# A two-layer decoder trunk on one core: another order of the MLP's first products, stores on other queues, one product earlier, one row turned later

## The chip, the cores and the metric

The kernel runs on one core of a Trainium2 chip. The core has TensorE (PE, matrix products), VectorE (DVE), ScalarE (ACT), GpSimd (POOL) and SyncE (SP, which here only issues DMAs). Each engine runs its own instructions in their order and waits for others by semaphores. The metric is the device time of one execution in microseconds (us), as the median of several.

## The reference

Two layers on 1024 tokens of width 1024. Layer 0 mixes tokens by attention (differential and forgetting heads), layer 1 by a gated linear recurrence. The change touches what follows the mixer in both:

```python
h = h + rmsnorm(m, ln_mix_post[layer])          # m: the mixer's output
u = rmsnorm(h, ln_mlp_pre[layer])
f = jnp.square(jax.nn.relu(u @ mlp_w_up[layer])) @ mlp_w_down[layer]   # 1024 -> 4096 -> 1024
h = h + rmsnorm(f, ln_mlp_post[layer])
e = rmsnorm(p[layer] @ ple_w_proj[layer], ple_norm[layer])
h = h + e * jax.nn.sigmoid(h @ ple_w_gate[layer])
```

## The kernel before

**Numbers.** Every float32 operand of a product is split into a high part (a cast on ACT, L122) and a low part (a subtraction on DVE, L123). `mm3` (L154 to L156) issues three matmuls per product: high by high, high by low, low by high. A weight is thus ready for its first matmul when ACT has cast it (`wAh`) and for its second when DVE has subtracted (`wAl`).

**The MLP** is computed with seven block products instead of eight: tokens, features and hidden columns are halved, and sums of blocks are multiplied. The names A11, A12, A22, S1 to S4 are weight blocks or sums of them; B11, B21, B22, T1 to T4 are the matching factors on the other side. `vec` (L887) makes the sums on DVE.

**End of the mixer** (`mix_out`, a plan written out by hand). `out_row` makes a row block of 128 tokens: product, norm, residual, norm. `combine` transposes it on PE and splits it and its combinations. In the gaps of the plan stand the *leads*: the first two products, A11 and A12, of the first three *Quads* (a Quad is 512 hidden columns), each 24 matmuls. For a Quad q, `first()` runs A11 into a bank and copies the bank on ACT (L1097); `second()` lets A12 add into the same bank and squares the result on ACT (L1080, L1081), and SP stores it (L1103). I call the halves a1, a2 (Quad 0), b1, b2, c1, c2; the prediction's c11 and c12 are c1 and c2. `early_sums` prepares S1 and S2 of Quad 0.

**Up stage** (`mlp_up`). For each of eight Quads the remaining products run (S1, S2, S4, S3, A22, or all seven). `keep` (L1152) stores each finished block of hidden values, 512 KB, in HBM (`hidD`): the three B blocks from ACT's squares, the four T blocks from DVE's subtractions. All stores and all loads go through SP's queue, in one order.

**Down stage** (`mlp_down`). Four chunks of two Quads each. `step` loads the hidden blocks into tiles `c` (L1267), splits them, and splits the weights; A22's weights for a chunk lie in one tile (`w22`, seen as `uh` in the trace). The seven products of a chunk run in the order A11, A12, S2, S3, A22, S1, S4 on two pairs of banks (`k0` to `k3`); `onto` adds a bank to the result X on DVE, in the first chunk it copies it on ACT (L1318); `temp` copies a bank to a tile M. In the last chunk `norms` (through `add_norm`) normalises finished rows and adds h, loaded by SP, and `turns` transposes them (L190) for the gate.

**Gate** (in `mlp_and_ple`). The product with the gate weights goes over eight row blocks: the first four, those normalised in `mlp_down`, first. `need_u` turns a row that isn't turned yet.

A scheduler orders each engine's instructions from the program's text before it runs. Its order is fixed on the chip.

Of the kernel before, what the change touches and what calls it, by code (L numbers as in the profile page):

```python
# [39 lines left out]
def tile_hybrid_trunk(  # L40
# [870 lines left out]
    class Layer:  # L911
# [6 lines left out]

        def add_norm(self, tb, g, a, ag, src, junk, small):

            h = row_tile()
            nc.sync.dma_start(out=h, in_=src)
            rs = rms_row(small, junk, a)
            vec(ag, a, g, ALU.mult)
            nc.vector.scalar_tensor_tensor(out=h, in0=ag, scalar=rs, in1=h, op0=ALU.mult, op1=ALU.add)
            return h


        def mix_out(self, wap, kpairs, src, part, order):
# [11 lines left out]
            with tc.tile_pool(name=f"pre{layer}", bufs=1, reuse_waits="tile") as mp:  # L941
# [66 lines left out]

                leads = []
                for q in range(NLEAD):  # L1010
                    leads += self.lead_steps(q, mp)
                plan = [(out_row, 0), (out_row, 1), (out_row, 2), (combine, 0), (out_row, 3), (combine, 1),
# [70 lines left out]
        def lead_steps(self, q, mp):  # L1083

            A = self.loader(self.up_view(q), lambda m, k: (wpool, "wraw", 2))
            slot = [mp if 2 * q < 3 else None, mp if 2 * q + 1 < 3 else None]
            st = {}

            def direct(name, n):
                wh, wl = self.weights({name: lambda: A(0, n)}, name, A, None, slot[n])  # L1090
                return wh, wl

            def first():
                a = st["A"] = pair_bank()
                self.up_product(a, direct("A11", 0), "A11", True, True)
                self.lead[q] = m1 = self.c.take()
                nc.scalar.copy(out=m1[1], in_=a)  # L1097

            def second():
                self.up_product(st["A"], direct("A12", 1), "A12", False, True)  # L1100
                c11 = row_tile()
                self.squared(c11, st["A"])
                nc.sync.dma_start(out=self.hidD[B11][q], in_=c11)  # L1103

            return [first, second]
# [9 lines left out]
        def mlp_up(self):  # L1115
            quads = FF // 512
            layer_ = self
            with tc.tile_pool(name=f"up{self.layer}", bufs=1, reuse_waits="tile") as hp:
# [10 lines left out]
                class Quad:  # L1129
# [21 lines left out]
                    def keep(self, i, t):  # L1151
                        nc.sync.dma_start(out=layer_.hidD[i][self.q], in_=t)  # L1152

# [135 lines left out]
        def mlp_down(self, macc, bank0, norms, turns):  # L1289
# [8 lines left out]
            for c in range(chunks):  # L1298
# [29 lines left out]
                for jj, b in product("A12", 1, True):  # L1328
                    onto((0, 0), jj, b)
                for jj, b in product("S2", 0, False):  # L1330
                    temp("u2", jj, b)
                    if c:
                        onto((1, 0), jj, M["u2", jj])
                for jj, b in product("S3", 0, False):
                    temp("u3", jj, b)
                    if c:
                        onto((1, 1), jj, M["u3", jj])
                for jj, b in product("A22", 0, False):
                    onto((0, 1), jj, b, True)
                    if final:  # L1340
# [8 lines left out]
                for jj, b in product("S4", 1, False):  # L1349
# [4 lines left out]
                    if final:  # L1354
                        turns(2 - jj)
            return rows

        def mlp_and_ple(self):
# [21 lines left out]
            normed = []  # L1380

            def norms(tbs, rows):
                if not gain:
# [3 lines left out]
                    quart[TA, 0] = (uh0, ul0)  # L1387
                    gain.append(macc.tile([P, 2, 512], F32, name="M", bufs=6).rearrange("p r d -> p (r d)"))
                for tb in tbs:
                    a = rows[tb]  # L1390
                    h = self.add_norm(tb, gain[0], a, a, hD[tb], gain[1], mp)
                    nc.sync.dma_start(out=hD[tb], in_=h)
                    normed.append((tb, h))

            def turns(n):
                for _ in range(n):
                    tb, h = normed.pop(0)
                    to_u(tb, h, self.down_bank(tb % 2))

# [13 lines left out]
            for nh in range(2):  # L1413
# [6 lines left out]
                for n, tb in enumerate(order):  # L1420
# [4 lines left out]
                    if nh == 0:  # L1425
                        need_u([order[n + 3]] if 1 <= n < 5 else [])
                    else:
                        drain(1)
# [81 lines left out]
```

## Time and profile before

| what | us |
|---|---|
| median of three runs | 2670.49 (2666.25 to 2670.78) |
| the profiled execution | 2666.86 |
| its span, first to last instruction | 2665.0 |
| PE busy in the span | 2512.3 (94%) |
| DVE, ACT, POOL busy | 1664.4, 1265.7, 221.1 |

The mean granted TensorE clock of the span is 0.976 of full speed. All times "at" in the rows are microseconds from the span's start. "Idle before" is the time in which an engine did nothing ahead of an instruction, and behind the arrow stands what released it. The touched places lie, in layer 0, at 736 to 770 (leads' end), 1050 to 1075 (start of the down stage) and 1350 to 1380 (turn to the gate); in layer 1, 1932 to 1966, 2236 to 2266 and 2540 to 2570.

### The profile page before, as it was taken

The page shows a single profiled execution, that of the slowest core. Times are in us where ns is not written, and L with a number is a line of the kernel's source. Part 1 is how long each engine was busy: PE and PEld are TensorE (multiplying, and loading weights), DVE is VectorE, ACT ScalarE, POOL GpSimd, SP SyncE. Part 2 cuts the span into 40 slices and gives each one's busy share as a digit, 9 for nine tenths or more (in the row PEclk, how much of TensorE's full clock was granted, in tenths as well). Part 3 has the DMA queues.
Part 4 walks back from the last instruction along what each step waited for, and adds up shares of the span by engine and source line. Part 5 has one row for each costly group of instructions (what it writes and reads, how often), then busy time and mean ns, then how long its engine had stood idle before and what let it go on. Part 6 is the DMA issues. An engine that isn't in the chain of part 4 may idle for free. (4 is left out here: it accounts for less than half of the span.)

```text
span 2665.0 us, 31196 instructions
## 1 busy us (share of the span) xinstructions
PE 2512.3 (94%) x11681; PEld 2046.6 (77%) x11681; DVE 1664.4 (62%) x2085; ACT 1265.7 (47%) x1867; POOL 221.1 (8%) x310
## 2 busy tenths in 40 slices
PE   8899999987889999999989999999889998999999
PEld 7687988765668887788877778877678886788877
DVE  5566766663777456677775455663876546677763
ACT  4455555653634445444443356662634444434431
POOL 1312223311100000000010000000100000000010
PEclk9999999999899999999999999999999999999999
DMA  4747543414655346444454322144655437444453
GB/s 160 204 140 209 154 141 115 151 68 182 233 166 206 135 157 246 150 150 142 142 197 143 126 83 71 59 144 170 241 178 182 150 135 257 153 150 142 146 186 111
DMA packets 231259, 417.91 MB, mean 157 GB/s; under 512 B 17075, under 2 KB 127772, under 8 KB 231108
## 3 DMA queue, kind: packets, MB, share of 16 engines
q1 hardware_dynamic: 215556, 393.37, 44.5%
q10 hardware_dynamic: 15552, 22.55, 2.3%
q8 instruction: 92, 1.51, 0.2%
q14 instruction: 59, 0.48, 0.1%
HBM read 290.40 MB, written 125.45 MB: 156 GB/s over the span
## 5 line engine op out<-in xcount | busy, mean ns | idle before, releaser
L122 ACT CAST wAh<-wq 128x1024 fp32r<-128x1024 f32 x114 | 119.6, 1049 | 306.8 <-PE k L156 159.5
L123 DVE TENSOR_TENSOR wAl<-wq,wAh 128x1024 fp32r<-128x1024 f32 x114 | 139.0, 1220 | 114.7 <-ACT wAh L122 114.7
L896 POOL TENSOR_TENSOR rs<-ms,nhalf 128x1 f32<-128x1 f32 x56 | 54.4, 976 | 1804.1 <-ACT ms L894 1804.0
L154 PE MATMUL sc<-uh,wAh 128*128 128x512 f32 x464 | 187.8, 405 | 14.0 <-ACT c L1097 7.0
L156 PE MATMUL sc<-uh,wAl 128*128 128x512 f32 x464 | 186.4, 402 | 3.1 <-DVE wAl L123 3.1
L155 PE MATMUL sc<-ul,wAh 128*128 128x512 f32 x464 | 186.4, 402 | 0.4 <-DVE ul L123 0.4
L155 PE MATMUL k<-wAl,ul 128*128 128x512 f32 x432 | 172.8, 400 | 13.8 <-DVE wAl L123 13.8
L156 PE MATMUL k<-wAh,ul 128*128 128x512 f32 x464 | 184.6, 399 | 0.0
L155 PE MATMUL k<-wAl,uh 128*128 128x512 f32 x464 | 183.9, 396 | 0.1
L154 PE MATMUL k<-wAh,uh 128*128 128x512 f32 x464 | 181.7, 397 | 1.6 <-ACT uh L122 1.6
L123 DVE TENSOR_TENSOR wAl<-wraw,wAh 128x1024 fp32r<-128x1024 f32 (+1 forms) x88 | 111.6, 1269 | 113.0 <-ACT wAh L122 112.6
L156 PE MATMUL k<-wAh,uh 128*128 128x512 f32 x432 | 171.3, 397 | 0.3 <-DVE uh L123 0.3
L154 PE MATMUL k<-wAh,ul 128*128 128x512 f32 x432 | 168.4, 397 | 1.5 <-ACT wAh L122 1.5
L122 ACT CAST wAh<-wraw 128x1024 fp32r<-128x1024 f32 (+1 forms) x88 | 92.1, 1048 | 163.2 <-PE sc L155 64.9
L154 PE MATMUL sc<-xh,wAh 128*128 128x512 f32 x384 | 152.0, 396 | 0.0
L155 PE MATMUL sc<-xl,wAh 128*128 128x512 f32 x384 | 151.6, 395 | 0.0
L156 PE MATMUL sc<-xh,wAl 128*128 128x512 f32 x384 | 151.1, 395 | 0.0
L154 PE MATMUL mm<-uh,wAh 128*128 128x512 f32 x312 | 126.8, 406 | 9.8 <-ACT st L349 8.7
L122 ACT CAST wAh<-S 128x1024 fp32r<-128x1024 f32 x60 | 63.0, 1050 | 151.7 <-PE k L156 76.7
L409 DVE CUSTOM_DVE_ANT_0 sn<-sc,bias 128x128 f32<-128x128 f32 (+7 forms) x128 | 94.5, 753 | 50.2 <-PE tp L426 18.8
L412 ACT ACTIVATE sn<-sn,nm 128x128 f32<-128x128 f32 (+7 forms) x128 | 99.2, 776 | 55.7 <-DVE nm L409 55.0
L155 PE MATMUL mm<-ul,wAh 128*128 128x512 f32 x312 | 124.4, 399 | 0.0
(414 smaller groups left out, 6695.0 us busy)
## 6 DMA issues: line engine op xcount, KB each, us to landing
c<-hid SPq DMA_DIRECT2D x112, 512.0 KB
hid<-t SPq DMA_DIRECT2D x48, 512.0 KB
wq<-in_mlp_w_up_dram SPq DMA_DIRECT2D x44, 512.0 KB
hid<-row SPq DMA_DIRECT2D x38, 512.0 KB
wraw<-in_mlp_w_up_dram SPq DMA_DIRECT2D x36, 512.0 KB
hD<-row SPq DMA_DIRECT2D x32, 512.0 KB
wq<-in_mlp_w_down_dram SPq DMA_DIRECT2D x32, 512.0 KB
hid<-c SPq DMA_DIRECT2D x26, 512.0 KB
```

The lines of the kernel that those rows point to most:

```text
L122: nc.scalar.copy(out=dst_h, in_=src)
L123: nc.vector.tensor_tensor(out=dst_l, in0=src, in1=f32(dst_h), op=ALU.subtract)
L154: nc.tensor.matmul(dst, lh, rh, start=start, stop=False, skip_group_check=onto)
L155: nc.tensor.matmul(dst, lh, rl, start=False, stop=False, skip_group_check=onto)
L156: nc.tensor.matmul(dst, ll, rh, start=False, stop=stop, skip_group_check=onto)
L409: nc.vector.tensor_tensor_reduce(out=sn[:, :w], in0=sps[:, :w], in1=bias, scale=-1.0, scalar=BIG, op0=ALU.add, op1=ALU.min, accum_out=nm)
L412: nc.scalar.activation(out=sn[:, :w], in_=sn[:, :w], func=AF.Exp, scale=-1.0, bias=nm, accum_out=z)
L896: nc.gpsimd.tensor_tensor(out=rs, in0=ms, in1=nhalf, op=ALU.pow)
```

## The change

Four edits, all in the MLP and in both layers:

1. The leads run as a1, a2, b1, c1, b2, c2 instead of a1, a2, b1, b2, c1, c2. The same three halves keep their weights in the extra tile.
2. The stores of B blocks (the leads' too) go on ACT's queue, those of T blocks on POOL's. SP issues loads, and of stores only those of other stages.
3. In the first chunk of the down stage A22 is the third product, on the second pair of banks. It starts C[0,1] by a copy on ACT, and S3's M is added there later on DVE, an add for each of two tiles.
4. In the last chunk one row less is turned before the gate: one behind S1 and one at each half of S4; the fourth is turned behind the gate's first row block. The h of the other four rows is loaded into M tiles instead of row tiles.

```diff
--- before.py
+++ after.py
@@ -916,9 +916,9 @@
                          for i in range(7)]
             self.uD = [dram.tile([P, D], F32, name=f"uD{layer}_{j}") for j in range(4)]
 
-        def add_norm(self, tb, g, a, ag, src, junk, small):
-
-            h = row_tile()
+        def add_norm(self, tb, g, a, ag, src, junk, small, new=row_tile):
+
+            h = new()
             nc.sync.dma_start(out=h, in_=src)
             rs = rms_row(small, junk, a)
             vec(ag, a, g, ALU.mult)
@@ -1006,9 +1006,8 @@
                     split(H[T4], L[T4], t4)
                     split(H[B22], L[B22], p2)
 
-                leads = []
-                for q in range(NLEAD):
-                    leads += self.lead_steps(q, mp)
+                a, b, c = (self.lead_steps(q, mp) for q in range(NLEAD))
+                leads = [a[0], a[1], b[0], c[0], b[1], c[1]]
                 plan = [(out_row, 0), (out_row, 1), (out_row, 2), (combine, 0), (out_row, 3), (combine, 1),
                         (out_row, 4), (combine, 2), (out_row, 5), (combine, 3), None, (combine, 4),
                         (out_row, 6), None, (combine, 5), (out_row, 7), None, None, (combine, 6), None,
@@ -1083,7 +1082,7 @@
         def lead_steps(self, q, mp):
 
             A = self.loader(self.up_view(q), lambda m, k: (wpool, "wraw", 2))
-            slot = [mp if 2 * q < 3 else None, mp if 2 * q + 1 < 3 else None]
+            slot = [mp if q < 2 else None, mp if q == 0 else None]
             st = {}
 
             def direct(name, n):
@@ -1100,7 +1099,7 @@
                 self.up_product(st["A"], direct("A12", 1), "A12", False, True)
                 c11 = row_tile()
                 self.squared(c11, st["A"])
-                nc.sync.dma_start(out=self.hidD[B11][q], in_=c11)
+                nc.scalar.dma_start(out=self.hidD[B11][q], in_=c11)
 
             return [first, second]
 
@@ -1149,7 +1148,7 @@
                         layer_.up_product(bank_, w, name, start, True)
 
                     def keep(self, i, t):
-                        nc.sync.dma_start(out=layer_.hidD[i][self.q], in_=t)
+                        (nc.gpsimd if i in (T1, T2, T3, T4) else nc.scalar).dma_start(out=layer_.hidD[i][self.q], in_=t)
 
                     def running(self, dst):
                         if self.led:
@@ -1327,16 +1326,18 @@
                     onto((0, 0), jj, b, True)
                 for jj, b in product("A12", 1, True):
                     onto((0, 0), jj, b)
+                if c == 0:
+                    for jj, b in product("A22", 1, True):
+                        onto((0, 1), jj, b, True)
                 for jj, b in product("S2", 0, False):
                     temp("u2", jj, b)
                     if c:
                         onto((1, 0), jj, M["u2", jj])
                 for jj, b in product("S3", 0, False):
                     temp("u3", jj, b)
-                    if c:
-                        onto((1, 1), jj, M["u3", jj])
-                for jj, b in product("A22", 0, False):
-                    onto((0, 1), jj, b, True)
+                    onto((1, 1) if c else (0, 1), jj, M["u3", jj])
+                for jj, b in product("A22", 0, False) if c else ():
+                    onto((0, 1), jj, b)
                     if final:
                         norms([4 * TA + 2 * jj + r for r in range(2)], rows)
                 for jj, b in product("S1", 1, True):
@@ -1352,7 +1353,7 @@
                     else:
                         vec(C[1, 0][jj], b, M["u2", jj], ALU.add)
                     if final:
-                        turns(2 - jj)
+                        turns(1)
             return rows
 
         def mlp_and_ple(self):
@@ -1379,23 +1380,26 @@
             gain = []
             normed = []
 
+            def m_tile():
+                return macc.tile([P, 2, 512], F32, name="M", bufs=6).rearrange("p r d -> p (r d)")
+
             def norms(tbs, rows):
                 if not gain:
                     gain.append(self.c.take()[1])
                     bcast_row(gain[0], ln_mlp_post[layer:layer + 1, :])
                     uh0 = up.tile([P, 4, 512], F32R, name=f"uh{TA}0")
                     quart[TA, 0] = (uh0, ul0)
-                    gain.append(macc.tile([P, 2, 512], F32, name="M", bufs=6).rearrange("p r d -> p (r d)"))
+                    gain.append(m_tile())
                 for tb in tbs:
                     a = rows[tb]
-                    h = self.add_norm(tb, gain[0], a, a, hD[tb], gain[1], mp)
+                    h = self.add_norm(tb, gain[0], a, a, hD[tb], gain[1], mp, row_tile if tb // 4 == TA else m_tile)
                     nc.sync.dma_start(out=hD[tb], in_=h)
                     normed.append((tb, h))
 
             def turns(n):
                 for _ in range(n):
                     tb, h = normed.pop(0)
-                    to_u(tb, h, self.down_bank(tb % 2))
+                    to_u(tb, h, self.down_bank(1 - tb % 2))
 
             rows = self.mlp_down(macc, bank0, norms, turns)
             close_psum()
@@ -1423,7 +1427,7 @@
                     need_u([tb])
                     tok_group(acc, tb, lambda kb: (w[kb // 2].h[:, kb % 2, :], w[kb // 2].l[:, kb % 2, :]))
                     if nh == 0:
-                        need_u([order[n + 3]] if 1 <= n < 5 else [])
+                        need_u([order[n + 3]] if n < 5 else [])
                     else:
                         drain(1)
                     eh = macc.tile([P, 2, 512], F32, name="M", bufs=6)
```

The instruction order that follows, at three places of layer 0. First DVE at the end of the leads. In the order before, `wAl_8343` holds the low weights of c2; `row_8243`, `u_` and `ul00` belong to the combine of row block 6.

```order
948 L887 TENSOR_TENSOR a_8297<-wraw_8295,a_8297 128x1024
949 L123 TENSOR_TENSOR wAl_8304<-wraw_8295,wAh_8303 128x1024
950 L123 TENSOR_TENSOR wAl_8308<-a_8297,wAh_8307 128x1024
951 L887 TENSOR_TENSOR row_8243<-tp_8233,row_8243 128x512
952 L123 TENSOR_TENSOR wAl_8343<-wraw_8340,wAh_8342 128x1024
953 L887 TENSOR_TENSOR u_8245<-tp_8238,row_8243 128x512
954 L123 TENSOR_TENSOR ul00_132<-row_8243,uh00_131 128x4x128
955 L887 TENSOR_TENSOR row_8243<-row_8243,u_8245 128x512
```

The same place on DVE now (`row_8242` is the former `row_8243`, `u_8244` the former `u_8245`):

```order
948 L181 SCALAR_TENSOR_TENSOR a_8118<-row_8148,rs_8163,gain_7582 128x1024
949 L887 TENSOR_TENSOR a_8297<-wraw_8295,a_8297 128x1024
950 L123 TENSOR_TENSOR wAl_8304<-wraw_8295,wAh_8303 128x1024
951 L123 TENSOR_TENSOR ul00_132<-row_8242,uh00_131 128x4x128
952 L887 TENSOR_TENSOR u_8244<-tp_8237,row_8242 128x512
953 L887 TENSOR_TENSOR u_8245<-tp_8237,u_8245 128x512
954 L123 TENSOR_TENSOR wAl_8308<-a_8297,wAh_8307 128x1024
955 L123 TENSOR_TENSOR wAl_8343<-wraw_8340,wAh_8342 128x1024
956 L887 TENSOR_TENSOR row_8242<-row_8242,u_8244 128x512
```

c2's low weights moved behind three steps of the combine, and the norm's last step `a_8118` behind the combine's first.

The second place is SP's queue at the end of the leads. `wraw` and `wq` are weight loads for Quads 0 and 1, `hid0_0_1` and `hid0_0_2` the stores of b's and c's squares. Before:

```order
278 L1060 DMA wraw_8444<-in_mlp_w_up_dram 128x4x256
279 L1103 DMA hid0_0_1_7479<-row_8229 128x1024
280 L1060 DMA wraw_8516<-in_mlp_w_up_dram 128x4x256
281 L1103 DMA hid0_0_2_7480<-row_8370 128x1024
282 L1060 DMA wq_8440<-in_mlp_w_up_dram 128x4x256
283 L1060 DMA wq_8442<-in_mlp_w_up_dram 128x4x256
284 L1060 DMA wq_8447<-in_mlp_w_up_dram 128x4x256
285 L1060 DMA wq_8514<-in_mlp_w_up_dram 128x4x256
```

Now, on the same queue:

```order
276 L995 DMA row_8321<-uD0_3_7537 128x1024
277 L1059 DMA wraw_8444<-in_mlp_w_up_dram 128x4x256
278 L1059 DMA wraw_8516<-in_mlp_w_up_dram 128x4x256
279 L1059 DMA wq_8440<-in_mlp_w_up_dram 128x4x256
280 L1059 DMA wq_8442<-in_mlp_w_up_dram 128x4x256
281 L1059 DMA wq_8447<-in_mlp_w_up_dram 128x4x256
282 L1059 DMA wq_8514<-in_mlp_w_up_dram 128x4x256
```

The stores are gone from SP, and the four `wq` loads follow the `wraw` loads.

The third place is DVE at the start of the down stage. Before, `wAl_10348` is the first half of S2's low weights; `S_` and `wq_` are weight sums, `uh` splits of hidden blocks or, in the sums, A22's weights:

```order
1124 L123 TENSOR_TENSOR uh00_10351<-c0_10352,uh00_10351 128x1024
1125 L887 TENSOR_TENSOR S_10129<-wraw_10341,uh10_10343 128x1024
1126 L887 TENSOR_TENSOR X00_10256<-k2_10284,X00_10256 128x2x512
1127 L887 TENSOR_TENSOR S_10130<-S_10129,wq_10131 128x1024
1128 L887 TENSOR_TENSOR S_10141<-wraw_10356,uh10_10343 128x1024
1129 L887 TENSOR_TENSOR wq_10131<-wq_10131,wraw_10341 128x1024
1130 L887 TENSOR_TENSOR wq_10267<-wq_10267,S_10130 128x1024
1131 L123 TENSOR_TENSOR uh01_10417<-c2_10418,uh01_10417 128x1024
1132 L887 TENSOR_TENSOR X01_10257<-k3_10310,X01_10257 128x2x512
1133 L887 TENSOR_TENSOR S_10142<-S_10141,wq_10143 128x1024
1134 L123 TENSOR_TENSOR wAl_10348<-S_10130,wAh_10347 128x1024
```

Now the third product is A22, with low weights `wAl_10344` and `wAl_10354`:

```order
1124 L887 TENSOR_TENSOR S_10129<-wraw_10414,uh10_10341 128x1024
1125 L123 TENSOR_TENSOR uh00_10347<-c0_10348,uh00_10347 128x1024
1126 L123 TENSOR_TENSOR wAl_10344<-uh10_10341,wAh_10343 128x1024
1127 L887 TENSOR_TENSOR S_10130<-S_10129,wq_10131 128x1024
1128 L887 TENSOR_TENSOR S_10141<-wraw_10427,uh10_10341 128x1024
1129 L887 TENSOR_TENSOR X00_10256<-k2_10284,X00_10256 128x2x512
1130 L887 TENSOR_TENSOR wq_10131<-wq_10131,wraw_10414 128x1024
1131 L887 TENSOR_TENSOR wq_10267<-wq_10267,S_10130 128x1024
1132 L123 TENSOR_TENSOR wAl_10354<-uh10_10341,wAh_10353 128x1024
1133 L887 TENSOR_TENSOR X01_10257<-k3_10310,X01_10257 128x2x512
```

The first half of A22's weights needs no sum and stands near the front of the chain, the second half two rows ahead of where S2's first half stood.

## Rows read from the trace of the kernel before

**Rows 1.** The page's first part: busy time, share of the span, instructions of each engine.

```profile
PE 2512.3 (94%) x11681; PEld 2046.6 (77%) x11681; DVE 1664.4 (62%) x2085; ACT 1265.7 (47%) x1867; POOL 221.1 (8%) x310
```

**Rows 2.** Windows: window, its length, engines' busy time (instructions), granted clock, DMA.

```profile
764.00:774.00 10.00, 6.76 (x18) 5.05 (x18) 9.78 (x10) 3.14 (x3) 0.00 (x0) 0.66 0.51 157
768.00:1040.00 272.00, 272.00 (x1156) 218.75 (x1157) 162.24 (x139) 123.67 (x121) 0.00 (x0) 0.99 0.50 173
1063.00:1074.00 11.00, 4.62 (x12) 3.38 (x13) 11.00 (x11) 3.41 (x4) 0.00 (x0) 0.69 0.49 157
1367.00:1378.00 11.00, 5.31 (x21) 4.22 (x22) 7.92 (x10) 5.71 (x10) 2.18 (x2) 0.69 0.74 251
1954.00:1966.00 12.00, 8.63 (x27) 6.12 (x26) 11.66 (x11) 3.14 (x3) 0.00 (x0) 0.72 0.45 136
2254.00:2266.00 12.00, 5.09 (x16) 3.52 (x14) 12.00 (x11) 4.00 (x5) 0.00 (x0) 0.72 0.51 167
```

**Rows 3.** Timeline of PE at the leads' end, layer 0: start, duration, [idle before, releaser].

```profile
741.97 0.50 PE L154 MATMUL sc<-uh,wAh 128*128 128x512 f32 x1 [3.49 <-ACT c L1097]
...
746.42 0.40 PE L154 MATMUL sc<-uh,wAh 128*128 128x512 f32 x1
746.65 0.39 PE L155 MATMUL sc<-ul,wAh 128*128 128x512 f32 x1
...
751.73 0.50 PE L154 MATMUL sc<-uh,wAh 128*128 128x512 f32 x1 [1.48 <-ACT row L1080]
...
765.64 0.50 PE L154 MATMUL sc<-uh,wAh 128*128 128x512 f32 x1 [2.44 <-ACT wAh L122]
...
767.97 0.80 PE L156 MATMUL sc<-uh,wAl 128*128 128x512 f32 x1 [1.60 <-DVE wAl L123]
```

**Rows 4.** Timeline of the same stretch: SP's queue and DVE.

```profile
753.17 0.32 SPq L1103 DMA_DIRECT2D hid<-row  x1
753.59 2.55 SPq L1060 DMA_DIRECT2D wq<-in_mlp_w_up_dram  x4
...
759.97 1.23 DVE L887 TENSOR_TENSOR S<-wq,wraw 128x1024 f32<-128x1024 f32 x1 [4.40 <-DMA wq<-in_mlp_w_up_dram]
```

**Rows 5.** Timeline at the start of the down stage: SP's queue, DVE, PE; last, layer 1.

```profile
1044.98 0.32 SPq L1152 DMA_DIRECT2D hid<-c  x1
...
1050.20 0.32 SPq L1267 DMA_DIRECT2D c<-hid  x1
...
1058.63 1.22 DVE L887 TENSOR_TENSOR S<-wraw,uh 128x1024 f32<-128x1024 f32 x1
...
1068.84 1.22 DVE L123 TENSOR_TENSOR wAl<-S,wAh 128x1024 fp32r<-128x1024 f32 x1
...
1063.52 0.73 PE L154 MATMUL k<-wAh,ul 128*128 128x512 f32 x2 [0.70 <-ACT wAh L122]
1070.11 0.80 PE L155 MATMUL k<-wAl,ul 128*128 128x512 f32 x1 [5.86 <-DVE wAl L123]
...
2261.98 0.79 PE L155 MATMUL k<-wAl,ul 128*128 128x512 f32 x1 [6.13 <-DVE wAl L123]
```

**Rows 6.** Timeline of POOL: the same small operation beside a busy and an idle DVE.

```profile
731.96 2.29 POOL L896 TENSOR_TENSOR rs<-ms,nhalf 128x1 f32<-128x1 f32 x1 [5.44 <-ACT ms L894]
...
1370.63 0.55 POOL L896 TENSOR_TENSOR rs<-ms,nhalf 128x1 f32<-128x1 f32 x1 [3.64 <-ACT ms L894]
```

**Rows 7.** Timeline at the turn to the gate: DVE, PE; last, layer 1.

```profile
1372.00 1.28 DVE L925 SCALAR_TENSOR_TENSOR row<-X,rs,row 128x1024 f32<-128x1024 f32 x1 [3.08 <-DMA row<-hD]
...
1373.94 1.12 PE L190 MATMUL k<-ident,row 128*128 128x128 f32 x4 [5.44 <-DVE ul L123]
...
2564.02 1.12 PE L190 MATMUL k<-ident,row 128*128 128x128 f32 x4 [3.66 <-DVE ul L123]
```

**Rows 8.** Timeline of ACT at the end of the up stage.

```profile
1048.81 1.05 ACT L122 CAST wAh<-wq 128x1024 fp32r<-128x1024 f32 x1 [6.37 <-PE k L156]
```

## The prediction

> **What bounds the kernel now.** I read four views, in this order. The page's first part says that PE is busy for 94% of the span [rows 1], so only PE's idle time and its slow-clock time can be won. The table by windows says where they are not: over the 272 us of the up stage PE is busy in all of them [rows 2]. So the stores that leave SP's queue there, and the work they add to other engines, are worth nothing in that stage. The other windows are the three touched places, and each shows idle time and a granted clock below 1: the end of the leads, the start of the down stage, the turn to the gate, once per layer. PE's timeline then gives each wait with its releaser, and the timelines of DVE and SP say what the releaser itself was late for.
>
> At full clock one 128x512 matmul follows the last after 0.233 us [rows 3], so a window's slow-clock loss is its busy time less its count times 0.233: leads 6.76 - 18 x 0.233 = 2.6 us, start of down 4.62 - 12 x 0.233 = 1.8 us, and in layer 1 8.63 - 27 x 0.233 = 2.3 us and 5.09 - 16 x 0.233 = 1.4 us [rows 2]. These windows hold the lower of the two clock levels, 1.2 instead of 2.4 GHz, each time behind an idle PE.
>
> **Leads.** Before, PE waits 3.49 us for the copy of c11's bank, 1.48 us for a square, then 2.44 and 1.60 us for the S4 weights of Quad 0 [rows 3].
> The first wait: with a 24-matmul half between c's two, the copy is long done when c12 starts. But DVE now writes c12's low weights behind three steps of the row combine that stood after them (the first pair of order fences), and ACT copies c11's bank ahead of row 7's norm. I walked DVE's new order by the durations of before: the low weights end some 3.7 us after PE could take them. One wait replaces the other: 0 us. From both sides: all 3.5 us and their slow clock (some 1.5 us, from the steps behind that wait) gone, or 2 us more.
> The square: a group of the last row's transposes now stands ahead of c12 on PE, and with it ACT's casts ahead of the square; I take 0.8 of the 1.48 us.
> The S4 weights: their chain starts at 759.97, when DVE's sum has waited 4.40 us for a load. That load was issued at 753.59, behind a store issued at 753.17 on the same queue, which waited for the square [rows 4]. Without the store the first two such loads go right behind the last of the raw weights, near 743, and the next two when PE frees their buffers, near 750 (second pair of order fences). The chain then starts when DVE ends the combine, not when data land, and ends near 762, where PE wants it. Gain: 2.44 + 1.60 + 2.6 of clock + 0.8, less 0.3 for what may remain: 7.1 us. In layer 1 the window is idle for 12.00 - 8.63 = 3.4 us and loses 2.3 us of clock [rows 2]; with 0.6 for the square and 0.3 off: 6.0 us. **Sum 13**, bounds 0 (loads held by their buffers as long as by the store) and 23 (first wait gone in both layers too).
>
> **Start of the down stage.** Before, PE waits 0.70 us for S2's high weights and 5.86 us for its low ones (6.13 us in layer 1) [rows 5]. Those close a chain on DVE from 1058.63 to the step that starts at 1068.84: nine steps of (1068.84 - 1058.63)/9 = 1.13 us. A22 needs no sums but the load itself, so third in the row it asks less. But two S2 matmuls still stand before its 48 on PE, so the 0.7 us stays, and its 8th matmul needs the second half's low weights, which DVE writes as the ninth step of the chain where S2's were the tenth (third pair of order fences). The chain can also begin a step sooner, near 1057.5, since the row uh00 now stands behind its first sum. The ninth step ends at 1057.5 + 8 x 1.13 + 1.22 = 1067.8; PE, from 1063.52 + 2 x 0.233 = 1064.0, reaches its matmul at 1065.7: a wait of 2.1 us. S2's own weights come 4.5 us behind, with 40 matmuls, 9.3 us, to cover them: hidden. That alone gains 5.86 - 2.1 = 3.8 us, and up to 1.8 us of clock.
> Against it: a load of the temporaries and the loads of A22's weights behind it on SP wait until a temporary's store has landed. On SP that store was issued at 1044.98 and the load released at 1050.20, 5.2 us later [rows 5]. Now POOL issues it. No row shows a store from POOL. From below, it costs what SP's does, 0.32 us to issue [rows 4]. From above, POOL's smallest operation takes 0.55 us beside an idle DVE and 2.29 us beside DVE steps with two SBUF inputs [rows 6], such as run when the last four temporaries are made; with that factor of 4 a store lands some microseconds later. I take 2 us later, near the low end since most of the way to landing is the transfer, which no engine slows: then 1.8 us are left per layer, with the clock drop kept. **Sum 3.5**, bounds +15 (all but the 0.7 us) and -29 (the last rival).
> The Trainium skill (SBUF — State Buffer, "SBUF: two separate sides") says that a DMA from the GpSimd queue has its descriptors written by that engine's cores, that a VectorE instruction in a two-port mode locks them out of the port they share, and that the same DMA from the ACT or SP queue is immune; for instructions with two SBUF inputs it limits the lock to GpSimd work that reads SBUF. [Rows 6] agree that POOL slows beside VectorE; no run here yet shows a POOL store. By the full lock the last rival holds, by the limited one the sum stands.
>
> **Turn to the gate.** Before, PE waits 5.44 us (3.66 us in layer 1) for the last transposes' low parts, and DVE had itself waited 3.08 us for a load of h [rows 7]. Now three rows are turned before the gate instead of four; the fourth comes behind the gate's first block, and h of the other four rows has tiles that are free early. What is late next: the third row's second half, whose DVE chain (two low parts, the norm's multiply-add, an accumulate, one low part, none over 1.28 us) ends near 1370.7 instead of 1373.94, of which 2.7 us are won in layer 0 and 1.3 in layer 1, where the wait was shorter. The clock drop I leave. **Sum 4**, bounds -2 (the gate's second block waits for the row turned later) and 14 (both waits and their clock).
>
> **Edits that I put at nothing.** ACT gets 27 stores per layer, each an issue of about 0.32 us as on SP [rows 4], some with a wait for an older transfer. At the end of the up stage ACT sat idle for 6.37 us until PE freed a weight buffer [rows 8]: it works that far ahead, and that hides an issue and its wait; if the cover goes, at most 27 x 0.32 = 9 us per layer. The two adds of M into C that A22's new place costs DVE, at 1.13 us, lie in the first chunk behind the wait, where PE never stops.
>
> **Sum.** 13 + 3.5 + 4 = 20.5 us off 2666.86 us for the profiled execution, 2646.4; off the median of the runs shown, 2670.49, it would be 2650. I say 2648.
>
> **Rivals.**
> 1. *More goes.* The copy's wait vanishes as well, stores land as before, and without long waits the clock stays up: 23 + 11 + 8 = 42 us, 2626. For it: the drops all stand behind waits of 2 us and more. Against: the low weights' new place on DVE.
> 2. *The waits only move.* The loads in the leads are held by their buffers, A22's weights land as late as S2's were ready; the turn's 4 us and 2 more stay: 6 us, 2661. For it: every chain at these places ends on DVE, which has one step after the other in the windows (9.78 us of 10.00 in the leads, 11.00 of 11.00 in down) [rows 2].
> 3. *Slower: POOL's stores starve.* The place is the end of the up stage: the last four temporaries' stores leave POOL one after the other, and the first copies into X and A22's loads wait for them. The second left SP at 1044.98 [rows 5]; with d us of issue for each, the fourth lands at 1044.98 + 3d + 5.2, and the two copies and the rest of DVE's chain take some 6 us more. With d = 10 that is 1086, 20 us after PE wants it at 1065.7. With the 0.7 us and 1.8 us of clock these are 22.9 us where before lost 0.7 + 5.86 + 1.8 = 8.4 us: 14.5 more per layer, and 2666.9 - 17 + 29 = 2679. It decides from d of about 8 us, where it eats the 17 us of the other places. Against it: 2.29 us is the worst row of a small operation [rows 6].
> That the change does not do what it says I count with 2.
>
> **How the numbers follow.** Forecast 0.52, more 0.19, waits move 0.16, slower 0.13. Faster and slower count from 0.2%, about 5.3 us, what a measurement of this kernel can tell from no change. The forecast's own range is 2638 to 2656; rival 2 lies at the line, and I count most of it as no change. Faster 0.52 + 0.19 + 0.05 = 0.76, of which I give 0.03 to no change for the spread of the runs; no change 0.14, slower 0.13. The range 2625 to 2668 takes in the first rival and the second whole and leaves the third out.
>
> **What would show it.** Right: in the leads no wait for S4 weights and no lower clock behind it, but a wait of 3 to 4 us before c12, now for DVE's low weights; at the start of down the wait near 2 to 4 us before A22's 8th matmul; at the turn 2 to 3 us less. Wrong: POOL rows of many microseconds or X copies far behind the last accumulation (rival 3), PE waits inside the up stage or the gate, or a first lead wait that is gone (rival 1).

## The result, and the profile after

The changed kernel takes 2639.64 us (median of 4 runs, 2637.07 to 2645.61) against 2668.37 us for the kernel before beside it (4 runs): ratio 0.990, 95% interval 0.9873 to 0.9926. The forecast was 2648 us. The profiled execution takes 2638.40 us, its span 2636.5 us, 28.5 us less than before.

The page's first line and its row for the new queue, against [rows 1]:

```profile
PE 2506.6 (95%) x11681; PEld 2042.1 (77%) x11681; DVE 1667.2 (63%) x2089; ACT 1266.5 (48%) x1867; POOL 261.5 (10%) x374
...
q0 software_dynamic: 9216, 33.56, 3.3%
```

PE is busy for 5.7 us less, because more of its work runs at full clock; the other 22.8 us are idle time. POOL's queue carries 33.56 MB, the 64 T blocks of the two layers.

Both programs issue PE's 11681 matmuls in nearly the same order, so the n-th matmul can be compared in the two traces, and a stage's gain is what the distance grows by across it (matmuls 3600 to 4000, 5000 to 5200 and 6200 to 6600 in layer 0; 8600 to 8800, 9600 to 10400 and 11000 to 11600 in layer 1). The sum is taken from the first matmul to the last, so it differs a little from the 28.5 us of the spans.

| stage | forecast, us | measured, us |
|---|---|---|
| leads, layer 0 and 1 | 7.1 + 6.0 | 8.7 + 8.2 |
| start of down | 1.8 + 1.7 | 3.6 + 4.8 |
| turn to the gate | 2.7 + 1.3 | 2.2 + 0.5 |
| everywhere else | 0 | 0.7 |
| sum | 20.5 | 28.7 |

The windows of the same places (columns as in [rows 2]):

```profile
736.00:749.00 13.00, 10.13 (x42) 7.54 (x40) 9.90 (x15) 7.96 (x11) 0.00 (x0) 0.87 0.69 216
764.00:774.00 10.00, 10.00 (x44) 7.86 (x43) 5.95 (x6) 2.10 (x2) 0.00 (x0) 1.00 0.56 183
1054.00:1064.00 10.00, 6.13 (x24) 4.41 (x25) 10.00 (x10) 2.08 (x3) 0.00 (x0) 1.00 0.53 179
1350.00:1366.00 16.00, 12.40 (x53) 9.76 (x52) 12.38 (x13) 6.93 (x15) 4.55 (x4) 0.79 0.42 165
1930.00:1946.00 16.00, 16.00 (x70) 12.90 (x69) 13.98 (x13) 4.21 (x4) 0.00 (x0) 1.00 0.46 150
2226.00:2236.00 10.00, 7.57 (x31) 5.18 (x29) 9.21 (x9) 6.03 (x7) 0.00 (x0) 1.00 0.63 238
```

At the S4 products of both layers (764 to 774, 1930 to 1946) and at the start of down (1054 to 1064, 2226 to 2236) the granted clock is 1.00, where [rows 2] had 0.66 to 0.72. The turn (1350 to 1366) and the stretch of c2's wait (736 to 749) still hold the lower level.

PE's waits in layer 0, at the leads, the start of down and the turn, against [rows 3], [rows 5] and [rows 7]:

```profile
738.65 0.50 PE L154 MATMUL sc<-uh,wAh 128*128 128x512 f32 x1 [0.47 <-ACT wAh L122]
...
741.34 0.80 PE L156 MATMUL sc<-uh,wAl 128*128 128x512 f32 x1 [1.96 <-DVE wAl L123]
...
749.23 0.50 PE L154 MATMUL sc<-uh,wAh 128*128 128x512 f32 x1 [0.68 <-ACT row L1079]
...
1055.95 0.74 PE L154 MATMUL k<-wAh,uh 128*128 128x512 f32 x2 [2.51 <-ACT wAh L122]
1057.09 0.50 PE L154 MATMUL k<-wAh,ul 128*128 128x512 f32 x1 [0.40 <-DVE X L887]
...
1060.49 0.50 PE L155 MATMUL k<-wAl,uh 128*128 128x512 f32 x1 [1.52 <-DVE wAl L123]
...
1353.67 0.66 PE L190 MATMUL k<-ident,row 128*128 128x128 f32 x4 [0.74 <-DVE ul L123]
1357.19 1.11 PE L190 MATMUL k<-ident,row 128*128 128x128 f32 x4 [2.86 <-DVE ul L123]
```

The S4 waits of 2.44 and 1.60 us are gone. c2 waits 0.47 and 1.96 us for its weights instead of 3.49 us for the copy. The 0.70 and 5.86 us before S2 became 2.51 us for the high weights of the two S2 matmuls, 0.40 us for an accumulation and 1.52 us for A22's second low weights. At the turn 5.44 us became 2.86 us.

The loads behind the S4 weights, on SP's queue, and the chain's start on DVE, against [rows 4]:

```profile
737.25 4.45 SPq L1059 DMA_DIRECT2D wraw<-in_mlp_w_up_dram  x2
741.79 20.11 SPq L1059 DMA_DIRECT2D wq<-in_mlp_w_up_dram  x7
```

```profile
753.23 1.22 DVE L887 TENSOR_TENSOR S<-wq,wraw 128x1024 f32<-128x1024 f32 x1
```

The `wq` loads go from 741.79 on, 11.8 us sooner by the span's time, and DVE's first sum, at 753.23, has no wait in front of it.

### The profile page after: what moved, and what is told of

It reads as the page before. It is cut to its first block, busy times and chain, and to the rows that moved or that the text cites. A ratio compares the mean times of both kernels' runs of the same rounds, so it can differ in the third digit from the quotient of the medians.

```text
span 2636.5 us, 31218 instructions
## 1 busy us (share of the span) xinstructions
PE 2506.6 (95%) x11681; PEld 2042.1 (77%) x11681; DVE 1667.2 (63%) x2089; ACT 1266.5 (48%) x1867; POOL 261.5 (10%) x374
## 3 DMA queue, kind: packets, MB, share of 16 engines
q0 software_dynamic: 9216, 33.56, 3.3%
q8 instruction: 92, 1.51, 0.2%
```

## The experiments

Differences by stage are read as above, in profiled executions. A second profile of the changed kernel differs from the first by up to 0.3 us at the leads and the start of down, but by 1.2 us in the turn and 1.1 us in the up stage of layer 1, and by some us in the stages ahead of the leads. At the start of down in layer 0 two runs with their edits elsewhere (the leads' order, the turns) still differ from the changed kernel by 1.0 us less and 1.1 us more. So a difference of about 1 us at the start of down or in the turn shows nothing by itself; the waits there say more.

One reason is the clock. In the second profile of the changed kernel, start of down in layer 0:

```profile
1057.64 1.22 PE L154 MATMUL k<-wAh,uh 128*128 128x512 f32 x2 [2.21 <-ACT wAh L122]
...
1062.18 0.50 PE L155 MATMUL k<-wAl,uh 128*128 128x512 f32 x1 [0.53 <-DVE wAl L123]
```

```profile
1055.00:1065.00 10.00, 7.26 (x23) 4.83 (x22) 10.00 (x10) 3.06 (x4) 0.00 (x0) 0.83 0.54 185
```

The same instructions met 2.51, 0.40 and 1.52 us of waits and a clock of 1.00 in the first profile; here the clock falls behind the first wait and is back before the second. A22's eighth matmul starts 7.1 us after the last matmul ahead of the waits, against 7.4 us in the first profile: DVE's low weights set that time, and slow matmuls ahead of the last wait only shorten it.

**Only the leads' stores moved, in the kernel before.**

```diff
-                nc.sync.dma_start(out=self.hidD[B11][q], in_=c11)
+                nc.scalar.dma_start(out=self.hidD[B11][q], in_=c11)
```

> The kernel before with one thing changed: the three stores of the leads' squares go on ACT's queue, nothing else. PE's order is that of before. Theory: the loads for the S4 weights leave SP some 10 us sooner and the waits of 2.4 and 1.6 us (1.9 and 1.5 us in layer 1) with the lower clock behind them are gone, 6 to 7 us per layer: about 2666 - 13 = 2653 us, with the waits of 3.5 and 1.5 us for the copy and the square as before. Rival, it takes the new order of the leads as well: 2664 us or more.

Measured: 2652.74 us (5 runs), ratio 0.9952 (0.9937 to 0.9968); leads 7.0 and 6.3 us less, nothing elsewhere from the start of down on beyond 0.5 us. Its PE and SP at the leads, layer 0:

```profile
739.94 0.50 PE L154 MATMUL sc<-uh,wAh 128*128 128x512 f32 x1 [3.49 <-ACT c L1097]
...
749.68 0.50 PE L154 MATMUL sc<-uh,wAh 128*128 128x512 f32 x1 [1.48 <-ACT row L1080]
```

```profile
740.74 21.38 SPq L1060 DMA_DIRECT2D wq<-in_mlp_w_up_dram  x7
```

PE's order is that of before, and so are the two waits ahead, 3.49 and 1.48 us; the S4 waits no longer stand behind them, and the loads leave from 740.74 on. Three stores per layer on another queue are about half of the whole gain. Up to the end of the leads PE, DVE and ACT run the same instructions in the same order as before, so the queue alone makes the difference.

**The leads' order undone** (in the changed kernel).

```diff
-                leads = [a[0], a[1], b[0], c[0], b[1], c[1]]
+                leads = [a[0], a[1], b[0], b[1], c[0], c[1]]
```

> The changed kernel with the first edit alone undone: the leads run a1, a2, b1, b2, c1, c2 again, the stores stay off SP. Theory: the 7 us per layer at the S4 weights come from the loads that no longer stand behind a store, so PE still has no wait and no lower clock there; only the 1.5 to 1.8 us at c's second half return (a wait of 3.5 us for the copy in place of about 2.4 us for weights). Expected about 2638 + 3 = 2641 us. Rival, the order of the leads makes the gain: the waits for the S4 weights (2.4 and 1.6 us in layer 0) and the lower clock come back, about 2638 + 16 = 2654 us.

Measured: 2639.52 us (4 runs), ratio 0.9906 (0.9888 to 0.9925), not to be told from the changed kernel by time. By the trace 1.6 us more in the leads of each layer; PE there:

```profile
740.09 0.62 PE L154 MATMUL sc<-uh,wAh 128*128 128x512 f32 x1 [3.50 <-ACT c L1096]
...
749.85 0.50 PE L154 MATMUL sc<-uh,wAh 128*128 128x512 f32 x1 [1.47 <-ACT row L1079]
```

The waits for the copy and the square are back as before, the S4 waits are not. The new order is worth 1.6 us per layer, and the rival falls.

**All stores back on SP** (in the changed kernel).

```diff
-                nc.scalar.dma_start(out=self.hidD[B11][q], in_=c11)
+                nc.sync.dma_start(out=self.hidD[B11][q], in_=c11)
...
-                        (nc.gpsimd if i in (T1, T2, T3, T4) else nc.scalar).dma_start(out=layer_.hidD[i][self.q], in_=t)
+                        nc.sync.dma_start(out=layer_.hidD[i][self.q], in_=t)
```

> The changed kernel with the second edit alone undone: all stores on SP's queue again. Theory: the leads lose the 7 us per layer at the S4 weights again (loads issued behind the store of the square), while at the start of the down stage the temporaries' store lands about 5.2 us after its issue instead of 7.3 us, so A22's weights come 2 us sooner: +7 -2 per layer, about 2638 + 10 = 2648 us. Rival, the stores' queue is worth nothing in the leads: no wait for S4 weights, and 2 us less per layer in down: 2634 us.

Measured: 2638.93 us (4 runs), ratio 0.9899 (0.9884 to 0.9914). The expected 2648 us was missed. The trace shows both parts: leads 5.7 and 4.5 us more, start of down 3.9 and 2.8 us less; I had put the second at 2 us, and it is not the queue's alone (next runs). PE at the leads and at the start of down, layer 0:

```profile
742.52 0.80 PE L156 MATMUL sc<-uh,wAl 128*128 128x512 f32 x1 [1.91 <-DVE wAl L123]
...
764.11 0.50 PE L154 MATMUL sc<-uh,wAh 128*128 128x512 f32 x1 [2.18 <-ACT wAh L122]
...
766.44 0.79 PE L156 MATMUL sc<-uh,wAl 128*128 128x512 f32 x1 [1.59 <-DVE wAl L123]
...
1062.91 0.73 PE L154 MATMUL k<-wAh,uh 128*128 128x512 f32 x2 [0.96 <-ACT wAh L122]
```

The first line is c2's wait, as in the changed kernel. The S4 waits are back, with 2.18 and 1.59 us. At the start of down one wait of 0.96 us is left of three. By time alone this run would say that the second edit is worth nothing; it is a gain and a loss of nearly one size.

**T stores on SP, on SP for the last Quad alone, on ACT** (in the changed kernel).

```diff
-                        (nc.gpsimd if i in (T1, T2, T3, T4) else nc.scalar).dma_start(
+                        (nc.sync if i in (T1, T2, T3, T4) else nc.scalar).dma_start(
```

```diff
+                        (nc.scalar if i in (B11, B21, B22) else nc.gpsimd if self.q < quads - 1 else nc.sync).dma_start(
```

```diff
+                        nc.scalar.dma_start(
```

> The changed kernel with the stores of the four T blocks on SP's queue instead of POOL's; the B blocks' stores stay on ACT's. Theory: a store from POOL lands 7.3 us after its issue against 5.2 us from SP, and at the start of the down stage this holds A22's weight loads and the copies into X; with SP the waits there are 1 us in place of 4 us, as in the run with all stores on SP, which won 3.9 and 3.1 us there; the leads keep their gain, since the store of the square is on ACT. Expected 7 us less than the changed kernel, 2631 to 2633 us. Rival: SP's loads at the start of down queue behind its own T stores again, as in the kernel before, and nothing is won: 2639 us.

> The changed kernel with the T stores of the last Quad alone on SP; the other 28 per layer stay on POOL. Theory: only the last four stores stand before something that PE waits for, so the whole gain of the run with all T stores on SP shows: 2631 to 2633 us, waits at the start of down of 1 us. Rival: the POOL stores cost time in the up stage, by the port that POOL and DVE share or by late tiles; then this run stays behind the run with all T stores on SP.

> The changed kernel with the T stores on ACT's queue. Theory: the stores land as fast as from SP, but ACT stands still until DVE has made each T block, so casts of weights and hidden blocks wait behind; in the up stage ACT is several us ahead and PE sees nothing; at the end of the up stage the casts for A12 are the next work and are not due before the T blocks are done. Expected 2631 to 2635 us. Rival: ACT's waits reach PE, with PE waits of 1 to 3 us in each Quad, 16 of them: 2650 us or more.

Measured: 2633.00 us, ratio 0.9875 (0.9861 to 0.9890); 2631.08 us, 0.9859 (0.9837 to 0.9881); 2633.69 us, 0.9878 (0.9864 to 0.9893), 4 runs each. Start of down: 4.0 and 2.5 us less, 3.9 and 3.2 us less, 3.5 and 2.6 us less. The leads' gain stays within 0.2 us in all three. First the chain in the changed kernel: POOL's store, the load on SP that waits for it, ACT's copy into X that waits for the last store, DVE's first sum:

```profile
1035.97 0.53 POOL L1151 DMA_DIRECT2D hid<-c  x1 [0.72 <-DVE c L887]
...
1043.27 0.32 SPq L1266 DMA_DIRECT2D c<-hid  x1
...
1047.27 1.93 ACT L1317 COPY X<-k 128x1024 f32<-128x1024 f32 x2 [3.96 <-DMA hid<-t]
...
1050.13 1.23 DVE L887 TENSOR_TENSOR S<-wraw,uh 128x1024 f32<-128x1024 f32 x1 [4.99 <-DMA uh<-in_mlp_w_down_dram]
```

Then the same store, load and sum with T stores on SP, and PE's one wait behind them:

```profile
1040.68 0.32 SPq L1151 DMA_DIRECT2D hid<-c  x1
...
1045.59 0.32 SPq L1266 DMA_DIRECT2D c<-hid  x1
...
1054.07 1.22 DVE L887 TENSOR_TENSOR S<-wraw,uh 128x1024 f32<-128x1024 f32 x1
...
1061.12 0.73 PE L154 MATMUL k<-wAh,uh 128*128 128x512 f32 x2 [0.96 <-ACT wAh L122]
```

From POOL the store's landing is waited for over 1043.27 - 1035.97 = 7.3 us, from SP 1045.59 - 1040.68 = 4.9 us, and ACT's copy waits 3.96 us for the last of the four. But the sooner landing is only a part of what these runs win. Measured against the same matmul of PE, the last one ahead of the waits (1053.05 in the changed kernel, 1058.13 with T stores on SP), DVE's first sum starts 2.9 us ahead of it from POOL and 4.1 us ahead from SP: 1.1 us sooner. A22's second low weights gain more, first in the changed kernel, then with T stores on SP:

```profile
1059.22 1.22 DVE L123 TENSOR_TENSOR wAl<-uh,wAh 128x1024 fp32r<-128x1024 f32 x1
...
1059.75 1.22 DVE L123 TENSOR_TENSOR wAl<-uh,wAh 128x1024 fp32r<-128x1024 f32 x1
```

They start 6.2 us behind that matmul in the one and 1.6 us behind it in the other, 4.6 us sooner. The other 3.4 us are three steps of DVE: in every run that takes the last T stores off POOL, the one with all stores on SP too, the scheduler wrote another order here, although the edit names only a queue. These weights are then the sixth step of DVE's chain instead of the ninth, and PE runs seven matmuls of A22 ahead of S2's two. So the 4 us are landing and order together; no run has the one order with the other queue, and the split stays open.

The run with only the last Quad's stores on SP wins the same. In layer 0's up stage no kernel with T stores on POOL loses anything against before; in layer 1's this run and the first profile of the changed kernel lose 1.0 and 1.1 us, the second profile none. On ACT's queue the stores do as well, and layer 0's up stage takes as long as before. POOL itself is not slow; from the changed kernel's trace:

```profile
L1151 POOL DMA_DIRECT2D hid<-t x48 | 25.9, 539 | 555.7 <-DVE t L887 555.7
...
hid<-t POOLq DMA_DIRECT2D x48, 512.0 KB, 4.7
```

An issue is 0.54 us beside DVE's two-input steps, not the 10 us of the last rival. The second line gives 4.7 us as the median from issue to landing, so 7.3 us is not what a store from POOL takes everywhere. Over all 64 it goes from 2.85 to 8.80 us: 2.85 to 3.52 us for the twelve between 883 and 967, right beside DVE's two-input steps, and 5.5, 7.3, 8.6 and 8.8 us for the last four of layer 0, which leave within 3.7 us. By the trace's DMA packets a store that lands in 2.85 us starts to move 1.1 us after its issue; these four start 2.6 to 5.8 us after theirs. What holds the packets back there, no run here tells.

**A22 fifth again** (in the changed kernel).

```diff
-                if c == 0:
-                    for jj, b in product("A22", 1, True):
-                        onto((0, 1), jj, b, True)
...
-                    onto((1, 1) if c else (0, 1), jj, M["u3", jj])
-                for jj, b in product("A22", 0, False) if c else ():
-                    onto((0, 1), jj, b)
+                    if c:
+                        onto((1, 1), jj, M["u3", jj])
+                for jj, b in product("A22", 0, False):
+                    onto((0, 1), jj, b, True)
```

> The changed kernel with the third edit alone undone: A22 is the fifth product of the first chunk again. Theory: PE again waits some 6 us in one piece for S2's low weights, now 2 us longer since the stores land later from POOL, with the lower clock behind it: the wait before the third product is 8 us, plus 1.8 us of clock, against 4.0 us in the changed kernel, so 5 to 6 us more per layer: about 2638 + 11 = 2649 us. Rival, the gain at the start of down comes from SP's free queue: the wait stays at 4 us or less, 2638 us.

Measured: 2652.94 us (4 runs), ratio 0.9949 (0.9933 to 0.9965); start of down 7.2 and 8.8 us more, nothing in the leads. PE and the window there, layer 0:

```profile
1053.85 0.72 PE L154 MATMUL k<-wAh,ul 128*128 128x512 f32 x2 [1.35 <-ACT wAh L122]
1058.44 0.80 PE L155 MATMUL k<-wAl,ul 128*128 128x512 f32 x1 [3.87 <-DVE wAl L123]
...
1066.39 0.50 PE L155 MATMUL k<-wAl,uh 128*128 128x512 f32 x1 [2.45 <-DVE wAl L123]
```

```profile
1050.00:1072.00 22.00, 14.32 (x43) 10.25 (x41) 17.47 (x16) 4.93 (x5) 0.00 (x0) 0.77 0.56 190
```

The waits are 1.35, 3.87 and 2.45 us, 7.7 us in all, about the 8 us expected, but in three pieces. The clock falls to 0.77 of the window, and its matmuls take 14.32 - 43 x 0.233 = 4.3 us more than at full clock. Of these, 2.7 us lie ahead of the last wait and 1.6 us behind it, where I had put 1.8.

**Four rows turned before the gate again** (in the changed kernel).

```diff
-                        turns(1)
+                        turns(2 - jj)
...
-                    h = self.add_norm(tb, gain[0], a, a, hD[tb], gain[1], mp, row_tile if tb // 4 == TA else m_tile)
+                    h = self.add_norm(tb, gain[0], a, a, hD[tb], gain[1], mp)
...
-                    to_u(tb, h, self.down_bank(1 - tb % 2))
+                    to_u(tb, h, self.down_bank(tb % 2))
...
-                        need_u([order[n + 3]] if n < 5 else [])
+                        need_u([order[n + 3]] if 1 <= n < 5 else [])
```

> The changed kernel with the fourth edit alone undone: four rows are turned before the gate, with row tiles for all h. Theory: the waits for the last transposes' low parts are 5.4 and 3.7 us again instead of 2.9 and 2.9 us: +2.2 us in layer 0, +0.5 us in layer 1, about 2641 us. Rival, the h loads were late because of SP's queue, which now holds no stores: the wait stays near 3 us and the time at 2638 us.

Measured: 2643.26 us (4 runs), ratio 0.9918 (0.9899 to 0.9936); the turn takes 1.8 and 0.5 us more, the second within the 1.2 us that two profiles of the changed kernel differ by. PE and DVE there, layer 0:

```profile
1354.24 1.25 PE L190 MATMUL k<-ident,row 128*128 128x128 f32 x8 [0.71 <-DVE ul L123]
1359.75 1.12 PE L190 MATMUL k<-ident,row 128*128 128x128 f32 x4 [4.25 <-DVE ul L123]
...
1357.80 1.28 DVE L925 SCALAR_TENSOR_TENSOR row<-X,rs,row 128x1024 f32<-128x1024 f32 x1 [1.90 <-DMA row<-hD]
```

PE's wait is 4.25 us, between the two sides: 1.2 of the 5.44 us of before went with the other edits, 1.4 us with this one. The 1.2 us are DVE's wait for h, 1.90 us here against 3.08 us before; why h lands sooner is not shown. The same wait of PE in layer 1 is 3.55 us, against 3.66 us before and 2.86 us in the changed kernel. By time alone this run is not told from the changed kernel.

**T stores on SP and c2's weights written ahead.**

```diff
+            def ahead():
+                st["w"] = direct("A12", 1)
...
-                self.up_product(st["A"], direct("A12", 1), "A12", False, True)
+                self.up_product(st["A"], st.get("w") or direct("A12", 1), "A12", False, True)
...
-            return [first, second]
+            return [first, second, ahead]
...
-                        lambda: self.early_sums(mp), (combine, 7), None]
+                        c[2], lambda: self.early_sums(mp), (combine, 7), None]
```

> T stores on SP as in the other run, and c2's weights written before the early sums in the program, so that DVE makes their low part one step (1.1 us) sooner. Theory: the wait of 2.4 us before c2 gets 1.1 us shorter per layer: 2 us less than the run with T stores on SP alone, 2629 to 2631 us. Rival: S2's low weights, which move behind, become late instead, and the time is the same.

> The changed kernel again, beside the next one on the same chip: 2639 us, ratio to before 0.99.

> T stores on SP and c2's weights ahead of the early sums, again with more rounds: by the trace of its first run 10 us less than the changed kernel (3 us per layer in the leads, 3 us per layer at the start of down, less some), about 2628 us, with an interval below that of the changed kernel. Rival: the first run was a lucky one in the attention part, and the two intervals overlap.

Measured: 2627.41 us, ratio 0.9860 (0.9840 to 0.9879), 4 runs; again 2625.47 us, 0.9845 (0.9828 to 0.9861), 5 runs, beside the changed kernel with 2638.63 us, 0.9896 (0.9879 to 0.9913), 4 runs. The two intervals do not meet: this version is faster than both kernels. Leads 3.2 and 3.0 us less than the changed kernel, start of down 3.1 and 2.8 us less. The window of the leads in layer 0, and PE's only wait in it:

```profile
728.00:748.00 20.00, 18.36 (x87) 14.48 (x87) 19.42 (x27) 15.79 (x26) 0.80 (x1) 1.00 0.74 238
```

```profile
744.35 0.66 PE L983 MATMUL tp<-ident,a 128*128 128x128 f32 x4 [1.59 <-ACT u L1000]
```

No wait for c2's weights is left and the clock stays at 1.00; the wait that remains is 1.59 us for a copy of the row combine. The expected 1.1 us in the leads was too little because the weights did not come one step sooner. DVE's row for c2's low weights, in the changed kernel and here:

```profile
740.07 1.22 DVE L123 TENSOR_TENSOR wAl<-wraw,wAh 128x1024 fp32r<-128x1024 f32 x1
...
729.12 1.22 DVE L123 TENSOR_TENSOR wAl<-wraw,wAh 128x1024 fp32r<-128x1024 f32 x1
```

They stand ahead of all early sums now, 9.9 us sooner against the same matmul of PE, and the scheduler moved the transposes around c2 on PE too.

## Why the prediction was right, and where it was off

- **The S4 weights** (forecast: 2.44 + 1.60 us of waits and 2.6 us of clock in layer 0, 3.4 and 2.3 in layer 1, less 0.3 each). Shown by the run with the leads' stores alone, which wins 7.0 and 6.3 us where the terms sum to 6.3 and 5.4. The mechanism, a load behind a store on one queue, held, and the size within a microsecond.
- **"One wait replaces the other: 0 us", and the square at 0.8 us.** The kind was right, the size not: the wait for c2's weights is 0.47 + 1.96 = 2.4 us, not 3.7, since DVE made them nearer to PE's need than my walk; the square's wait fell by 0.8 us. Together the trace has 1.8 and 2.0 us, and undoing the order costs 1.6 per layer.
- **The start of down, sum 3.5, measured 8.4** (8.9 by the second profile). This is the step that was off. The failed term is "with the clock drop kept", 1.8 and 1.4 us: after the change no slow matmul stands behind the last wait, whether the clock stayed up (both layers in the first profile) or fell and came back ahead of that wait (layer 0 in the second). The other 1.6 us are layer 1's waits, 0.77 + 6.13 us before against 1.66 + 0.40 + 1.51 us, a gain of 3.3 us where 1.7 was put. In layer 0 the waits were sized about right in total, 0.7 + 2.1 + 2 = 4.8 us forecast and 2.51 + 0.40 + 1.52 = 4.4 measured, but that is luck: the wait before S2's two matmuls was to stay at 0.7 us and grew, and the one before A22's eighth matmul was to be 2 to 4 us and is 1.52 us.
- **The price of POOL's stores** was argued to be late landing, not a slow engine. The issue is indeed only 0.54 us, and the store named in the prediction lands 7.3 - 5.2 = 2.1 us later, as put. The reason given does not hold: by the trace's DMA packets the transfer itself is 2.5 of the 7.3 us, and 3.2 go by before its first packet. What the price is as a whole stays open, since the runs that take the stores off POOL win 3.9 and 2.8 us with another instruction order at the same time. The Trainium skill's lock (SBUF — State Buffer, "SBUF: two separate sides") does not show for these steps with two SBUF inputs, in line with the limit that the page gives.
- **The turn, sum 4, measured 2.7.** The wait is 2.86 us in both layers, where the third row's chain is late next as forecast, step by step; the lower clock stayed. Layer 1 had only 3.66 us to lose, and its 0.5 us is within what two profiles differ by.
- **Edits put at nothing.** ACT's queue got 24 stores per layer, not 27, and layer 0's up stage takes as long as before, so this term held there.
- **The rivals.** Rival 1 did not come as it stands, for c2's wait is there; the version with c2's weights ahead and T stores on SP is near to what it described, and its 2625 to 2627 us lie where it was priced, 2626. That is partly luck: it priced 23 + 11 + 8 us, and the second profile of that version has 22.6, 15.6 and 2.5 us. Rival 2 falls with the S4 waits, rival 3 with the 0.54 us.

## What to carry to other kernels

A load that stands behind a store in one queue leaves when the store's data are ready: look for the store ahead of the load before reordering compute, and move only the few stores that stand before something that is waited for. When two edits of a change pull in opposite ways, the total tells nothing: compare the same instruction's place in both traces, stage by stage. An edit that names only a queue can change the instruction order too: compare the orders before a gain is put down to the queue. And count a lower clock only behind the last wait of a place; ahead of a wait it only shortens that wait.

## What the runs showed that I had not expected

The lower clock does not follow from the waits alone. The same program at the same place kept 1.00 behind waits of 2.51, 0.40 and 1.52 us in one profile and fell behind 2.21 us in the other. Behind 1.35, 3.87 and 2.45 us the window had 0.77, and behind 0.47 and 1.96 us at the leads 0.87.

At the start of down a store of 512 KB issued by POOL was waited for over 7.3 us and the same one issued by SP over 4.9 to 5.2 us, while the issues differ by only 0.2 us. In a quiet stretch a store from POOL landed after 2.85 us.
